# Squares queued in the first quad, weights a block ahead and a feature-major second down projection in a two-layer decoder

## The chip, the cores and the metric

The kernel runs on one core of a Trainium2 chip. The metric is device time in microseconds (us) of one execution. The engines are named as in the profile: PE is TensorE's matmuls, PEld its weight loads, DVE is VectorE, ACT is ScalarE, POOL is GpSimd, SP is SyncE, which issues most DMAs. Every engine works through its own queue in the order that was fixed when the program was built.

## The reference

A decoder trunk of two layers over 512 positions of 1024 features, in float32. Each layer adds a mixer's output and then a gated feed-forward to the residual stream x:

```
x = x + mix @ w_out[layer]
x = x + swiglu(rmsnorm(x, ffn_norm_g[layer]), w_gate_up[layer], w_down[layer])

def swiglu(h, w_gate_up, w_down):
    g, u = jnp.split(h @ w_gate_up, 2, axis=-1)
    return (jax.nn.silu(g) * u) @ w_down
...
return rmsnorm(x, final_norm_g)
```

The hidden width of the feed-forward is 2816. Layer 0 mixes with forgetting attention, layer 1 with differential attention; both add cross-attention into 256 memory tokens. The change touches neither attention.

## The kernel before

Float32 products are made of three products: an operand is split into a high part (a cast on ScalarE, `split` at L228) and the rest (a subtraction on VectorE, L229), and hi x hi, lo x hi and hi x lo are summed in PSUM. Activations lie feature-major (128 features on partitions, 512 positions along the row), in eight blocks kb; `xh`, `xl` hold the split parts of the stream.

After the mixer of a layer, `output_and_ffn` runs two parts.

`out_proj` (L588) makes the output projection in four blocks o of two feature blocks each. `project` (L187) loads the weights of a block in four chunks, splits each (`chunk`, L173; for chunks 0 and 4 the low part is added up by a DMA from POOL's queue) and issues 48 products of 512 columns. Behind them comes the block's epilogue: two adds of the residual on VectorE (L603, L604), a scaled copy on ScalarE (L608), and `Quarters.make` (L560), which forms sums and differences of quarters (s2, s3, s4) and splits all of them for the products of the feed-forward. In layer 0 the squares of the new stream are added up there as well (`squares`, L231). In layer 1 each feature block is turned to position-major rows instead, by four transposes on TensorE and a copy on ScalarE (`turn_rows`, L616), because layer 1's last norm and output are by position. `ahead`, called ahead of block 3, loads and splits the first three weight tiles of the feed-forward (`FirstThree`, L819).

`ffn` (L828) makes gate and up products in 11 groups of 256 hidden features ("quads"), each by a seven-product scheme over quarters instead of eight (`product`, L832: 24 products of 256 columns each). `first_quad` (L852) starts with the three products whose operands need no weight sums. The norm of the stream comes late, as a factor r1 that `activate` (L898) multiplies in before and after Silu. In layer 0 r1 is made by `finish_norm` (L262) from one total over partitions, issued behind the first three products; in layer 1 by `row_squares` (L622) and `norm_of_rows` (L627), issued behind the a22 product. `gate` (L904) multiplies, splits and stores the gated block `ah`, `al`.

The down projection of earlier quads fills the later ones: `down_blocks` (L961) makes eight pieces for each group of quads, `quad` (L910) places four of them between its products (`fill`). In layer 0 a piece is 12 products of 512 columns with the weights standing in the array, feature-major (L986 to L988), added to the residual by L990. In layer 1 a piece is 24 products of 256 columns with the activations standing, position-major (L977 to L979), added to the rows by L982. The last group of layer 1 is `final` (L1019): products, residual, final norm and output for four tiles of 128 positions.

The order of instructions on each engine is fixed by a list scheduler: among the instructions that are ready by its own model of time, the one written first in the program goes first. Instructions written inside `with behind(engine)` (L104) cannot stand ahead of the engine's last instruction written so far.

Of the kernel before, what the change touches and what calls it, by code (L numbers as in the profile page):

```python
# [34 lines left out]
def tile_yoco(  # L35
# [151 lines left out]
    def project(segs, gain, ah, al, outs, nkb, n=S, order=None, by_dma=()):  # L187

        starts = order or list(range(0, nkb, CK))
        for kb0 in starts:  # L190
            nk = min(CK, nkb - kb0)
            hi, lo = chunk(segs, kb0, nk, gain, kb0 in by_dma)
# [345 lines left out]
    class Quarters:  # L538


        def __init__(self, pl):
            self.sh = pl.tile([P, NP, 3 * H], F32R, tag="sh", name=nm("sh"))
            self.sl = pl.tile([P, NP, 3 * H], F32R, tag="sl", name=nm("sl"))
            self.x = pl.tile([P, 4 * D], F32, tag="res", name=nm("res"))
# [4 lines left out]
        def rows(self):  # L549
            return self.x.rearrange("p (t d) -> p t d", t=NT)  # L550
# [21 lines left out]
    class Scratch:  # L572


        def __init__(self, pl):
            self.pl, self.n = pl, 0
# [7 lines left out]
        def next_half(self):  # L584
            self.n += 1
            return self.half(("p1", "u2", "u3")[self.n % 3])

    def out_proj(l, yh, yl, order, qs, sc, ahead):  # L588

        acc = tmp("xacc")  # L590
        late, xg = [], None
        for o in range(4):
            bs = two_banks(("acc", "sc", "y", "tr")[o])
            if o == 3:
                ahead()
            project([(w_out[l], o * 256, 256)], None, yh, yl, bs, NKB, order=order, by_dma=(0, 4))
            for f in late:
                f()
# [15 lines left out]
        return acc, late  # L614

    def turn_rows(kb, xn, rows):  # L616
        b = bank("tr")
        for t in range(NT):
            pe.transpose(b[:, t * P : (t + 1) * P], xn[:, t * P : (t + 1) * P], ident)
        act.copy(rows[:, :, kb * P : (kb + 1) * P], b.rearrange("p (t c) -> p t c", c=P))  # L620

    def row_squares(rows, ss, half):  # L622
        for t in range(NT):
            q = work()
# [651 lines left out]
```

## Time and profile before

| | |
|---|---|
| median of 3 runs | 1194.24 us (1193.36 to 1194.33) |
| the profiled execution | 1194.78 us |
| its span, first to last instruction | 1193.0 us |
| granted TensorE clock, mean over the span | 0.994 |
| busy: PE, PEld, DVE, ACT, POOL | 1164.1, 1062.2, 993.7, 662.6, 158.9 us |

Busy time is the union of an engine's instructions. The profiled execution has 1.78 us around its span. A matmul's row shows its start and its modelled duration; matmuls overlap, so the time that one costs is read from its start to the start of the next.

### The profile page before, as it was taken

Reading aid. Unit: us, or ns where it says so; the run is one execution under the profiler, and the core shown is the slowest. Engines: PE = TensorE matmul, PEld = TensorE weight load, DVE = VectorE, ACT = ScalarE, POOL = GpSimd, SP = SyncE. Lnnn points to the kernel's source line nnn. Section 1 sums busy time; section 2 is a strip of 40 time slices with the busy share of each in tenths; the row PEclk is TensorE's granted clock in tenths of the full one; section 3 lists DMA queues with packets and bytes.
Section 4 is the critical chain, followed back from the end, with each engine's and each line's share of the span. In section 5 each row is a group of like instructions: output and inputs, shape, how many; then the busy total and the mean of one; then the engine's idle time right before and its main releaser. Section 6 shows DMA issues by size and latency. Waiting matters only on the chain.

```text
span 1193.0 us, 21037 instructions
## 1 busy us (share of the span) xinstructions
PE 1164.1 (98%) x7866; PEld 1062.2 (89%) x7866; DVE 993.7 (83%) x1705; ACT 662.6 (56%) x1206; POOL 158.9 (13%) x154
## 2 busy tenths in 40 slices
PE   8999999999999999999999999998999999999997
PEld 7888888789999999999987878876999999999996
DVE  5879987799987787888779999979798887877776
ACT  7658776775444333344466878887554343333334
POOL 0002001113121111110001020111221111111000
PEclk8999999999999999999999999999999999999999
DMA  7533334458777666664233335346778666665512
GB/s 239 140 88 83 78 76 103 130 128 190 187 182 167 152 156 155 155 145 120 72 109 99 86 86 148 105 111 150 159 174 199 164 151 145 158 150 146 148 54 89
DMA packets 163065, 160.46 MB, mean 134 GB/s; under 512 B 12993, under 2 KB 152698, under 8 KB 162962
## 3 DMA queue, kind: packets, MB, share of 16 engines
q1 hardware_dynamic: 136146, 130.79, 37.0%
q0 software_dynamic: 26240, 27.27, 15.8%
q8 instruction: 62, 1.02, 0.4%
q10 hardware_dynamic: 576, 1.05, 0.2%
q14 instruction: 41, 0.34, 0.1%
HBM read 142.23 MB, written 2.10 MB: 121 GB/s over the span
## 4 chain that ended last, share of the span: by engine, by line
PE 75%; DVE 13%; ACT 5%; DMA 3%; issue 2%; SPq 1%; DVEq 0%; ACTq 0%; POOL 0%; POOLq 0%
PE acc L842 4%; PE acc L841 4%; PE y L842 4%; PE y L841 4%; PE y L840 4%; PE acc L840 4%; PE tr L986 3%; PE tr L987 3%; PE tr L988 3%; PE sc L842 3%; PE sc L841 3%; PE sc L840 3%; PE tr L979 3%; PE tr L977 3%; PE tr L978 3%; PE acc L201 3%
## 5 line engine op out<-in xcount | busy, mean ns | idle before, releaser
L228 ACT CAST fhi<-raw 128x1024 fp32r<-128x1024 f32 (+1 forms) x202 | 208.2, 1034 | 277.1 <-PE sc L842 107.6
L229 DVE TENSOR_TENSOR flo<-raw,fhi 128x1024 fp32r<-128x1024 f32 (+1 forms) x202 | 241.1, 1198 | 32.7 <-ACT fhi L228 32.7
L799 POOL DMA_DIRECT2D raw<-in_w_gate_up_dram x88 | 106.3, 1420 | 467.1 <-DMA raw<-in_w_gate_up_dram 256.8
L170 ACT ACTIVATE whi<-raw,gains 128x256 fp32r<-128x256 f32 (+1 forms) x192 | 86.7, 503 | 37.3 <-PE acc L201 20.2
L171 DVE SCALAR_TENSOR_TENSOR wlo<-raw,gains,whi 128x256 fp32r<-128x256 f32 (+1 forms) x192 | 87.4, 495 | 16.5 <-ACT whi L170 14.9
L842 PE MATMUL acc<-xl,fhi 128*128 128x256 f32 x352 | 99.2, 282 | 0.0
L840 PE MATMUL acc<-xh,fhi 128*128 128x256 f32 x352 | 99.0, 281 | 0.0
L841 PE MATMUL acc<-xh,flo 128*128 128x256 f32 x352 | 98.6, 280 | 0.1
L979 PE MATMUL tr<-flo,ah 128*128 128x256 f32 x288 | 81.3, 282 | 0.0
L977 PE MATMUL tr<-fhi,ah 128*128 128x256 f32 x288 | 81.3, 282 | 0.0
L978 PE MATMUL tr<-fhi,al 128*128 128x256 f32 x288 | 81.0, 282 | 0.0
L841 PE MATMUL y<-sh,flo 128*128 128x256 f32 x256 | 72.3, 283 | 3.4 <-DVE flo L229 3.4
L842 PE MATMUL y<-sl,fhi 128*128 128x256 f32 x256 | 72.7, 284 | 0.3 <-DVE sl L229 0.2
L840 PE MATMUL y<-sh,fhi 128*128 128x256 f32 x256 | 72.2, 282 | 0.0
L986 PE MATMUL tr<-ah,fhi 128*128 128x512 f32 x176 | 69.3, 394 | 0.7 <-ACT ah L228 0.7
L987 PE MATMUL tr<-ah,flo 128*128 128x512 f32 x176 | 69.1, 393 | 0.0
L988 PE MATMUL tr<-al,fhi 128*128 128x512 f32 x176 | 68.8, 392 | 0.0
L841 PEld LDWEIGHTS acc<-xh,flo 128*128 128x128 f32 x352 | 66.5, 189 | 0.8 <-DVE flo L229 0.3
L840 PEld LDWEIGHTS acc<-xh,fhi 128*128 128x128 f32 x352 | 66.5, 189 | 0.6
L842 PEld LDWEIGHTS acc<-xl,fhi 128*128 128x128 f32 x352 | 66.4, 189 | 0.5 <-DVE xl L229 0.4
L199 PE MATMUL acc<-xh,whi 128*128 128x512 f32 x168 | 66.6, 397 | 0.2 <-DVE qk L732 0.2
L200 PE MATMUL acc<-xh,wlo 128*128 128x512 f32 x168 | 66.3, 395 | 0.0
(494 smaller groups left out, 3788.8 us busy)
## 6 DMA issues: line engine op xcount, KB each, us to landing
raw<-in_w_gate_up_dram SPq DMA_DIRECT2D x220, 256.0 KB, 3.4
raw<-in_w_gate_up_dram POOLq DMA_DIRECT2D x88, 256.0 KB, 5.8
raw<-in_w_down_dram SPq DMA_DIRECT2D x80, 256.0 KB, 3.5
raw<-in_w_out_dram SPq DMA_DIRECT2D x32, 256.0 KB, 2.7
raw<-in_a_w_in_dram SPq DMA_DIRECT2D x48, 128.0 KB, 2.4
raw<-in_w_kv_shared_dram SPq DMA_DIRECT2D x24, 256.0 KB, 3.3
raw<-in_w_mem_kv_dram SPq DMA_DIRECT2D x16, 256.0 KB, 3.3
raw<-in_a_w_in_dram SPq DMA_DIRECT2D x16, 256.0 KB, 4.0
```

Of the source, the lines that this page charges most:

```text
L228: act.copy(h, src)
L229: dve.tensor_sub(l, src, f32(h))
L799: pool.dma_start(t[:, k : k + 2], plus[:, k : k + 2], accum_op=ALU.add)
L840: pe.matmul(o, hi[:, e, uc], ah, start=u == 0 and e == 0, stop=False)
L841: pe.matmul(o, lo[:, e, uc], ah, start=False, stop=False)
L842: pe.matmul(o, hi[:, e, uc], al, start=False, stop=u == 1 and e == NP - 1)
L977: pe.matmul(o, h[:, tc_], hi[:, k], start=t % 2 == 0 and k == 0, stop=False)
L978: pe.matmul(o, l_[:, tc_], hi[:, k], start=False, stop=False)
L979: pe.matmul(o, h[:, tc_], lo[:, k], start=False, stop=t % 2 == 1 and k == nk - 1)
L986: pe.matmul(b, hi[:, k, oc], h, start=k == 0, stop=False)
L987: pe.matmul(b, lo[:, k, oc], h, start=False, stop=False)
L988: pe.matmul(b, hi[:, k, oc], l_, start=False, stop=k == nk - 1)
```

## The change

- `out_proj`: the weights of block o + 1 are loaded and split behind block o's products and ahead of its epilogue; `ahead` is called behind the weights of block 3, ahead of block 2's epilogue. Both layers keep the stream feature-major in `qs.block(kb)`; the transposes and the row squares are gone from here, and so are the squares of layer 0.
- `first_quad`: the first three products are queued behind all of TensorE's earlier instructions. The eight squares of the stream (ScalarE) are queued behind the copy of v1, with their adds on VectorE; `finish_norm` is queued behind the a22 products, in both layers.
- `down_blocks`: layer 1 takes layer 0's form, 12 products of 512 columns in a piece.
- The end of layer 1: the eight feature blocks are turned to rows there, four transposes and four copies of 128x128 each, into two tiles that take the places of `sh` and `sl`.

```
-    def project(segs, gain, ah, al, outs, nkb, n=S, order=None, by_dma=()):
+    def project(segs, gain, ah, al, outs, nkb, n=S, order=None, made=None):
...
-            hi, lo = chunk(segs, kb0, nk, gain, kb0 in by_dma)
+            hi, lo = made[kb0] if made else chunk(segs, kb0, nk, gain)
...
-        def rows(self):
-            return self.x.rearrange("p (t d) -> p t d", t=NT)
+        def make_rows(self):
+
+            return [self.pl.tile([P, 2, D], F32, tag=t, name=nm("row")) for t in ("sh", "sl")]
...
-        acc = tmp("xacc")
-        late, xg = [], None
+
+        def weights(o):
+            return {kb: chunk([(w_out[l], o * 256, 256)], kb, CK, None, kb in (0, 4)) for kb in order}
+
+        made = weights(0)
         for o in range(4):
             bs = two_banks(("acc", "sc", "y", "tr")[o])
-            if o == 3:
+            project(None, None, yh, yl, bs, NKB, order=order, made=made)
+            if o < 3:
+                made = weights(o + 1)
+            if o == 2:
                 ahead()
-            project([(w_out[l], o * 256, 256)], None, yh, yl, bs, NKB, order=order, by_dma=(0, 4))
-            for f in late:
-                f()
-            late = []
+            xg = sc.full("g")
             for j in range(2):
                 kb = 2 * o + j
-                xn = qs.block(kb) if l == 0 else sc.next_half()
-                dve.tensor_add(xn, bs[j], f32(xh[:, kb]))
-                dve.tensor_add(xn, xn, f32(xl[:, kb]))
-                if j == 0:
-                    xg = sc.full("g")
+                dve.tensor_add(qs.block(kb), bs[j], f32(xh[:, kb]))
+                dve.tensor_add(qs.block(kb), qs.block(kb), f32(xl[:, kb]))
                 g = gains[:, G_FFN[l] + kb : G_FFN[l] + kb + 1]
-                act.activation(xg[:, j], xn, AF.Copy, scale=g)
-                if l == 0:
-                    squares(xn, acc, kb == 0)
-                else:
-                    late.append(lambda kb=kb, xn=xn: turn_rows(kb, xn, qs.rows()))
+                act.activation(xg[:, j], qs.block(kb), AF.Copy, scale=g)
...
+        def turn_rows(i, rows):
+            b = bank("sc")
+            for t in range(NT):
+                pe.transpose(b[:, t * P : (t + 1) * P], qs.block(i)[:, t * P : (t + 1) * P], ident)
+            for t in range(NT):
+                act.copy(rows[t // 2][:, t % 2, i * P : (i + 1) * P], b[:, t * P : (t + 1) * P])
...
             bp1, bp2, bp3 = bank("acc"), bank("sc"), bank("y")
-            for es in (range(NP - 1), range(NP - 1, NP)):
-                product(bp1, "a11", w.w11, es)
-                product(bp2, "a12", w.w21, es)
-                product(bp3, "s4", w.w22, es)
+            with behind(pe):
+                for es in (range(NP - 1), range(NP - 1, NP)):
+                    product(bp1, "a11", w.w11, es)
+                    product(bp2, "a12", w.w21, es)
+                    product(bp3, "s4", w.w22, es)
             t1 = raw(w.b12, w.b11)
             wt3 = parts(w.t3)
-            with behind(pe):
-                if last:
-                    for f in late:
-                        f()
-                    row_squares(qs.rows(), ss, 1)
-                else:
-                    finish_norm(acc, False, bank("tr"))
...
             act.copy(v1, halves(bp3))
+            acc = tmp("xacc")
+            with behind(act):
+                for i in range(NKB):
+                    squares(qs.block(i), acc, i == 0)
...
             product(bp4, "a22", wt4)
-            if last:
-                with behind(pe):
-                    norm_of_rows(ss)
+            with behind(pe):
+                finish_norm(acc, False, bank("tr"))
...
-                if last:
-                    for t in (2 * (i % 2), 2 * (i % 2) + 1):
-                        tc_, o = slice(t * P, (t + 1) * P), b[:, (t % 2) * H : (t % 2) * H + H]
-                        for k, (h, l_) in enumerate(a):
-                            pe.matmul(o, h[:, tc_], hi[:, k], start=t % 2 == 0 and k == 0, stop=False)
-                            pe.matmul(o, l_[:, tc_], hi[:, k], start=False, stop=False)
-                            pe.matmul(o, h[:, tc_], lo[:, k], start=False, stop=t % 2 == 1 and k == nk - 1)
-                    t0 = 2 * (i % 2)
-                    dst = qs.rows()[:, t0 : t0 + 2, c * 256 : c * 256 + 256]
-                    dve.tensor_add(dst, halves(b), dst)
-                    return
...
-        final(w, blocks_of(GROUPS[-1]), qs.rows(), ring, sc)
-
-    def final(w, a, xtok, ring, sc):
+        rows = qs.make_rows()
+        for i in range(NKB):
+            turn_rows(i, rows)
+        final(w, blocks_of(GROUPS[-1]), rows, ring, sc)
+
+    def final(w, a, rows, ring, sc):
...
-                dve.tensor_add(xo[:, c], o, xtok[:, t, c])
+                dve.tensor_add(xo[:, c], o, rows[t // 2][:, t % 2, c])
```

## Rows read from the trace of the kernel before

**Rows 1.** The page, first part: busy us, share of the span, instructions.

```profile
PE 1164.1 (98%) x7866; PEld 1062.2 (89%) x7866; DVE 993.7 (83%) x1705; ACT 662.6 (56%) x1206; POOL 158.9 (13%) x154
```

**Rows 2.** Windows by stage: length, busy us of each engine (instructions), granted clock, DMA share, GB/s.

```profile
257.27:268.42 11.15, 11.15 (x49) 9.02 (x48) 10.50 (x17) 5.41 (x8) 0.86 (x1) 1.00 0.27 49
268.42:289.53 21.11, 20.96 (x172) 20.27 (x171) 19.11 (x29) 12.52 (x17) 7.24 (x6) 1.00 0.95 218
289.53:588.67 299.14, 298.46 (x2114) 279.88 (x2113) 248.98 (x265) 120.38 (x123) 44.08 (x40) 1.00 0.62 152
...
819.53:840.44 20.91, 16.88 (x76) 13.36 (x75) 14.88 (x25) 11.97 (x24) 1.74 (x2) 0.92 0.34 73
840.44:860.34 19.90, 19.86 (x167) 19.55 (x166) 15.82 (x26) 14.11 (x26) 7.24 (x6) 1.00 0.98 226
860.34:1163.96 303.62, 303.55 (x2554) 303.34 (x2553) 250.41 (x271) 122.15 (x125) 43.47 (x36) 1.00 0.60 147
1163.96:1193.00 29.04, 22.56 (x110) 18.42 (x108) 18.34 (x46) 13.53 (x33) 0.00 (x0) 0.93 0.25 91
```

**Rows 3.** Windows around TensorE's longest stop in layer 1, and one of the start.

```profile
10.00:20.00 10.00, 8.04 (x51) 7.36 (x50) 6.47 (x21) 9.88 (x26) 1.28 (x5) 0.77 0.82 281
...
822.40:826.10 3.70, 0.28 (x2) 0.07 (x1) 3.70 (x8) 3.70 (x10) 0.00 (x0) 1.00 0.00 0
826.10:828.00 1.90, 1.73 (x6) 1.24 (x7) 1.90 (x4) 1.90 (x5) 0.00 (x0) 0.72 0.35 97
828.00:830.00 2.00, 2.00 (x6) 1.52 (x6) 2.00 (x4) 1.32 (x4) 0.88 (x1) 0.50 0.51 170
830.00:832.00 2.00, 2.00 (x9) 1.37 (x7) 2.00 (x4) 0.60 (x1) 0.86 (x1) 0.91 0.76 131
```

**Rows 4.** Timeline of PE: a whole down piece and the product behind it, both layers.

```profile
580.23 0.40 PE L986 MATMUL tr<-ah,fhi 128*128 128x512 f32 x1
...
583.03 0.27 PE L840 MATMUL acc<-sh,fhi 128*128 128x256 f32 x1
...
1138.41 0.28 PE L977 MATMUL tr<-fhi,ah 128*128 128x256 f32 x1
...
1141.24 0.28 PE L840 MATMUL sc<-sh,fhi 128*128 128x256 f32 x1
```

**Rows 5.** Waits of PE, 811.5 to 875: us in total, times, longest.

```profile
PE y L841 <- DVE flo L229: 3.4, 1, 3.4
...
PE tr L200 <- DMA wlo<-raw: 0.4, 1, 0.4
```

**Rows 6.** Timeline of PE: the total, transposes, and the small norm products.

```profile
277.55 1.02 PE L253 MATMUL tr<-xacc,ones 128*128 128x512 f32 x2
...
278.53 0.28 PE L840 MATMUL acc<-sh,fhi 128*128 128x256 f32 x1
...
819.53 0.60 PE L619 MATMUL tr<-ident,p 128*128 128x128 f32 x4
...
820.32 0.37 PE L840 MATMUL acc<-xh,fhi 128*128 128x256 f32 x1
...
861.78 1.05 PE L637 MATMUL tr<-work,ones 128*128 128x128 f32 x8
862.59 0.36 PE L840 MATMUL acc<-xh,fhi 128*128 128x256 f32 x1
```

**Rows 7.** The line that adds squares up: duration ns min/median/max, first and last start.

```profile
L238 DVE TENSOR_TENSOR xacc<-xacc,work x14: 683/686/692, 243.0 to 613.5; 128x512 f32<-128x512 f32 x14
```

**Rows 8.** Timeline of DVE and PE, layer 0: r1, its first use, first down product.

```profile
287.23 0.41 DVE L265 TENSOR_SCALAR r<-work 128x512 f32<-128x512 f32 x1
...
290.49 1.22 DVE L900 TENSOR_TENSOR g<-g,r 128x1024 f32<-128x1024 f32 x1
...
299.18 0.50 PE L986 MATMUL tr<-ah,fhi 128*128 128x512 f32 x1 [0.68 <-ACT ah L228]
```

**Rows 9.** Groups by line and form, ACT: busy us, mean ns; idle before.

```profile
L467 ACT CAST vp<-vmem 128x128 fp32r<-128x128 f32 x8 | 1.9, 294 | 0.1
```

More of the change, by code (lines that the diff above doesn't have):

```diff
@@ L541, in __init__ @@
         def __init__(self, pl):
+            self.pl = pl
             self.sh = pl.tile([P, NP, 3 * H], F32R, tag="sh", name=nm("sh"))
@@ L575, in __init__ @@
         def __init__(self, pl):
-            self.pl, self.n = pl, 0
+            self.pl = pl
         def half(self, tag):
@@ L613, in out_proj @@
-            qs.make(o, xg, sc.full("u").rearrange("p a c -> p (a c)")[:, : 3 * H])
[L614 to L624, printed above, removed]
-            act.activation(q, rows[:, t, half * S : half * S + S], AF.Square, accum_out=ss[:, half, t : t + 1])
@@ L627, in norm_of_rows @@
-    def norm_of_rows(ss):
-        r = tmp("nrm", (P, NT))
-        dve.tensor_add(ss[:, 0], ss[:, 0], ss[:, 1])
-        rstd(ss[:, 0], NT, D, r)
-        dve.tensor_scalar_mul(r, r, undo_k(D))
-        d = work().rearrange("p (t c) -> p t c", c=P)
-        b = bank("tr")
-        for t in range(NT):
-            dve.tensor_scalar_mul(d[:, t], ident, r[:, t : t + 1])
-            pe.matmul(b[:, t * P : (t + 1) * P], ones, d[:, t], start=True, stop=True)
-        act.copy(r1, b)
+                dve.tensor_add(qs.block(kb), bs[j], f32(xh[:, kb]))
@@ L826, in __init__, with ffn @@
             self.w11, self.w21, self.w22 = (ring.parts(t) for t in (self.raw11, self.raw21, self.raw22))
-    def ffn(l, acc, last, qs, late, ring, sc, pl, ahead):
+    def ffn(l, last, qs, ring, sc, pl, ahead):
         raw, parts = ring.load, ring.parts
@@ L847, in ffn @@
         gated = {}
-        if last:
-            ss = tmp("ss", (P, 2, NT))
-            row_squares(qs.rows(), ss, 0)
+        def turn_rows(i, rows):
[4 more added lines that the diff above has]
+                act.copy(rows[t // 2][:, t % 2, i * P : (i + 1) * P], b[:, t * P : (t + 1) * P])
         def first_quad(w):
             bp1, bp2, bp3 = bank("acc"), bank("sc"), bank("y")
-            for es in (range(NP - 1), range(NP - 1, NP)):
-                product(bp1, "a11", w.w11, es)
-                product(bp2, "a12", w.w21, es)
-                product(bp3, "s4", w.w22, es)
+            with behind(pe):
[3 more added lines that the diff above has]
+                    product(bp3, "s4", w.w22, es)
             t1 = raw(w.b12, w.b11)
             wt3 = parts(w.t3)
-            with behind(pe):
-                if last:
-                    for f in late:
-                        f()
-                    row_squares(qs.rows(), ss, 1)
-                else:
-                    finish_norm(acc, False, bank("tr"))
             p1, u2, u3 = sc.half("p1"), sc.half("u2"), sc.half("u3")
@@ L972, in piece @@
                 b = bank("tr")
-                if last:
-                    for t in (2 * (i % 2), 2 * (i % 2) + 1):
-                        tc_, o = slice(t * P, (t + 1) * P), b[:, (t % 2) * H : (t % 2) * H + H]
-                        for k, (h, l_) in enumerate(a):
-                            pe.matmul(o, h[:, tc_], hi[:, k], start=t % 2 == 0 and k == 0, stop=False)
-                            pe.matmul(o, l_[:, tc_], hi[:, k], start=False, stop=False)
-                            pe.matmul(o, h[:, tc_], lo[:, k], start=False, stop=t % 2 == 1 and k == nk - 1)
-                    t0 = 2 * (i % 2)
-                    dst = qs.rows()[:, t0 : t0 + 2, c * 256 : c * 256 + 256]
-                    dve.tensor_add(dst, halves(b), dst)
-                    return
                 oc = slice((i % 2) * P, (i % 2) * P + P)
@@ L1062, in output_and_ffn @@
             ahead = []
-            acc, late = out_proj(
+            out_proj(
                 l, yh, yl, [6, 0, 2, 4], qs, sc, lambda: ahead.append(FirstThree(l, ring))
@@ L1068, in output_and_ffn @@
             ring.far = open_pool(fs, f"f{l}", "right")
-            acc = ffn(l, acc, last, qs, late, ring, sc, open_pool(fs, f"a{l}"), ahead)
+            acc = ffn(l, last, qs, ring, sc, open_pool(fs, f"a{l}"), ahead)
         if not last:
```

3 lines of the change are left out of this document (removed).

## The prediction

> **What bounds the kernel now.** I read the page's first part, then the windows by stage, then the timeline inside the stages where TensorE stops. TensorE is busy nearly all of the span [rows 1], so a change pays only by fewer or faster products, or by removing a stop of TensorE. The windows show where stops are [rows 2]. The reader is to see two pairs. Quads 1 to 10 of layer 0 (289.53 to 588.67) and of layer 1 (860.34 to 1163.96) make the same gate and up products and the same down sum; only the form of the down products differs, and the second stretch is longer. The last block of the output projection in layer 0 (257.27 to 268.42) is filled without a gap; in layer 1 the corresponding stretch (819.53 to 840.44) has TensorE idle for 4.03 us and a granted clock of 0.92. VectorE is idle there too, for 6.03 us, so it is not simply too slow: its work comes in the wrong order. The waits name it: the product of the first quad waits 3.4 us for the fhi/flo split of its weights [rows 5], at the head of TensorE's queue, and the products of block 3 stand behind it. [...]
>
> **The change, part by part.** Sums are made against the profiled execution, 1194.78 us (span 1193.0 and 1.78 around it); the median of the runs is 0.54 lower.
>
> **Down products of layer 1.** 864 products of 256 columns become 432 of 512. Busy time of TensorE in the ten quads is 303.55 us in layer 1 and 298.46 in layer 0 [rows 2]; 0.81 of the first is the eight small norm products (861.78 to 862.59) [rows 6]. 303.55 - 0.81 - 298.46 = 4.3 us. A single whole piece says less: 24 narrow products take 1138.41 to 1141.24, 2.83 us, 12 wide ones 580.23 to 583.03, 2.80 us [rows 4]; over 36 whole pieces (32 and eight half ones) that is 1.1 us. I take 4.3, since it is the same stage end to end, and keep 1.1 as the bound. The adds after them stay 40, of the same number of elements, and w_down's loads stay as they are: nothing, hidden under TensorE.
>
> The rows show 118 ns from one narrow product to the next and 233 ns for a wide one [rows 4]. [...]
>
> **The transition in layer 1.** Three edits meet here: weights of the next block are made before the block's own epilogue; the first quad's products are queued behind all of the projection, so that none can stand before block 3; and the 32 transposes, their copies and the row squares leave this stretch. TensorE's account of the gain: 4.03 us idle, 0.08 of 20.91 us for the clock, 1.7 us [rows 2, 3], and the transposes: eight of them take 819.53 to 820.32, 0.79 us, so 32 take 3.2, with their switches 3.3 us [rows 6]. Together 9.0 us. VectorE's account: it is idle 6.03 us in 819.53 to 840.44 and 4.08 in 840.44 to 860.34 [rows 2], 10.1 together; the change adds seven adds of squares of 0.69 us [rows 7], 4.8, and a norm over 512 columns, three operations of that shape and one of 0.41, 2.5 us. If the removed narrow ones count for nothing, 10.1 - 7.3 = 2.8 us are left. Those are the bounds, 2.8 and 9.0. I take 6.0, between them: VectorE's surplus can flow into the quads, where it idles 53 of 303.62 us, but the epilogue of block 3 can only start when block 3 is done, and the last block of first products waits for it. What is late next is therefore the split of block 3's operands (sl), ahead of the s4 products.
>
> **The norm product.** One total over 512 columns (277.55 to 278.53, 0.98 us) stands in place of the eight small ones, 0.81 us [rows 6]: +0.2.
>
> **Layer 0.** The squares move from the epilogue onto ScalarE's queue behind the copy of v1, and the total moves behind the a22 products, from 277.55 to about 286.7 (2.83 us of s1 products ahead of 289.53). On ScalarE the splits of wt4, t1 and quad 1's weights stand behind eight squares; on VectorE their adds. The norm r1 is done at 287.6 now and its first use starts at 290.49, so 2.9 us of cover exist; TensorE waits 0.68 us already where the first down piece needs the gated block [rows 8]. From total to r1 the operations alone need about 5 us, so r1 comes at about 291.7, 1.2 us after the present first use. Bounds: 0, where other products of quad 1 are put ahead of the down piece, and 6.3, the present 10.1 us from total to r1 begun at 286.7. I take 0.5, near the first, since layer 1 already runs with its norm that late [rows 6] and its stage is filled [rows 2]. The weights made ahead give nothing in layer 0: its blocks run without idle, hidden by the projection's own products. On SP's and POOL's queues the loads of block 3 of w_out and the two lo parts added by DMA move ahead of those of FirstThree; their 0.4 us wait [rows 5] is in the idle time above.
>
> **The end.** The transposes now stand between the last adds of the down sum and the final products, on the path: +3.3 us. Their 32 copies on ScalarE can only start when the s4 products of quad 10 release sh and sl, and hold two banks. The nearest row of 128x128 is 294 ns [rows 9], so 9.4 us against 2.8 us of the last down piece and 3.3 of transposes; final products stand ready to fill the gap. Nothing more is counted, up to 3.3 us where they do not fill it.
>
> Sum: -4.3 - 6.0 + 0.2 + 0.5 + 3.3 = -6.3, so 1188.5 for the profile and about **1188.0 us** for the runs. With each gain at its better bound and layer 0 at 0 it is 1184.5.
>
> **Rivals.** A: VectorE bounds the transition (gain 2.8, not 6.0): 1191.1 us. For it: the flo split ends TensorE's long wait there; against: 10 us of VectorE idle. B: the wide products gain 1.1 only: 1191.1 us. For it the single pieces, against it the stage. C: the copies at the end hold TensorE 3.3 us: 1191.2 us. D, on the other side: r1 is late at the first down piece of quad 1 in both layers, because the squares and their adds precede the weights' splits and TensorE's order leaves the piece in its place. Place: the wait of the first down product. Price: 6.3 us each in place of my 0.5, so 1200.0; the two waits must exceed 6.8 us together to decide. For it: 0.68 us are lost there now; against: layer 1 passes the place filled. E: the clock falls in the transposes at the end. In 10 to 20 us, where transposes and waits alternate, the granted clock was 0.77 [rows 3]; a fall cost 1.7 us at 826: 1189.7. [...] F: A and B together: 1194.3, so the change does nothing.
>
> **How the numbers follow.** Forecast 0.48, A 0.16, B 0.10, C 0.07, D 0.08, E 0.07, F 0.04. A measurement here tells about 0.2% (2.4 us) from no change. Faster takes the forecast, E, and about two thirds of A, B and C, which lie 0.7 us beyond that line: 0.77. Same takes the rest of these and F: 0.15. Slower is D: 0.08. The likeliest case has its own range of 1184.5 to 1191; the whole range, 1184.0 to 1193.0, leaves out D, F and a little of the low side.
>
> **What would show it.** Right: no TensorE idle over 2 us between the projection of layer 1 and its first quad, clock 1.00 there; the ten quads of layer 1 some 4 us shorter; 32 transposes after the last down piece, with final products among them. Wrong: a wait of the first down product of quad 1 on the gated block's split of several us (D), a wait of transposes on ScalarE's copies (C), or idle before the s4 products of layer 1 on sl of more than 4 us (A).

## The result, and the profile after

The changed kernel takes **1207.35 us** (median of four runs, 1203.79 to 1208.12); the kernel before, run beside it, 1194.03 us. The ratio is 1.0099, 95% interval 1.0085 to 1.0112: about 12 us slower by the ratio (13.3 us between these two medians), where 6 us faster were forecast. The profiled execution took 1208.12 us, with a span of 1206.0.

The first part of the page after, beside [rows 1]. TensorE has 438 instructions fewer and is nevertheless 6.4 us longer busy:

```profile
PE 1170.5 (97%) x7428; PEld 1047.9 (87%) x7428; DVE 999.4 (83%) x1707; ACT 664.8 (55%) x1221; POOL 158.3 (13%) x154
```

The windows by stage after, in the order of [rows 2] and with its columns: block 3 of the projection and first quad of layer 0; then, behind the rows left out, block 3 and first quad of layer 1; its ten quads; the end.

```profile
257.10:268.17 11.07, 11.07 (x49) 8.93 (x48) 7.39 (x13) 5.54 (x8) 0.86 (x1) 1.00 0.22 53
268.17:294.13 25.96, 24.69 (x199) 23.80 (x198) 24.16 (x36) 15.47 (x24) 7.27 (x6) 1.00 0.81 182
...
823.87:843.42 19.55, 14.19 (x51) 11.02 (x50) 13.18 (x22) 10.91 (x16) 2.93 (x3) 0.83 0.43 89
843.42:870.65 27.23, 24.33 (x173) 22.02 (x172) 24.85 (x37) 15.64 (x23) 7.24 (x6) 0.94 0.77 175
870.65:1173.04 302.39, 300.88 (x2112) 282.00 (x2112) 249.22 (x267) 121.21 (x124) 43.44 (x36) 1.00 0.59 147
1173.04:1206.00 32.96, 26.41 (x141) 21.74 (x139) 18.57 (x46) 19.19 (x65) 0.00 (x0) 0.96 0.22 80
```

The first quad of layer 1 was filled before (19.86 of 19.90 us); now it stands 2.9 us still and has a clock of 0.94. Block 3 ahead of it stands 5.4 us still, at 0.83. The end has grown by 3.9 us. The waits of TensorE from 811.5 to 890 us name the places, as [rows 5] did before:

```profile
PE tr L200 <- DMA wlo<-raw: 5.4, 1, 5.4
PE y L809 <- ACT fhi L228: 2.1, 3, 0.9
PE tr L253 <- DVE xacc L238: 0.8, 1, 0.8
PE tr L946 <- ACT ah L228: 0.6, 1, 0.6
PE acc L809 <- ACT fhi L228: 0.6, 1, 0.6
PE sc L809 <- ACT fhi L228: 0.4, 1, 0.4
```

The stop of the kernel before was a split of VectorE. In its place there is a longer one, on a low part that DMA adds up (`wlo<-raw`). Everything below it is new: the first quad waits for splits of its weights, for the sum of squares and for the gated block. The timeline of ScalarE in the first quad of layer 1 shows why:

```profile
856.60 0.59 ACT L843 COPY u<-y 128x512 f32<-128x512 f32 x1 [2.14 <-PE y L811]
857.09 0.64 ACT L234 ACTIVATE xacc<-res 128x512 f32<-128x512 f32 x1
857.62 3.75 ACT L237 ACTIVATE work<-res 128x512 f32<-128x512 f32 x7
861.27 2.92 ACT L228 CAST fhi<-raw 128x1024 fp32r<-128x1024 f32 x3
```

Eight squares stand for 4.2 us ahead of three casts of weights. TensorE's timeline there (in brackets the idle time before and what ended it) has two stops for those casts and one for the sum; the rows between are left out:

```profile
863.30 0.38 PE L809 MATMUL acc<-xh,fhi 128*128 128x256 f32 x1 [0.56 <-ACT fhi L228]
...
864.24 0.39 PE L809 MATMUL y<-sh,fhi 128*128 128x256 f32 x1 [0.56 <-ACT fhi L228]
...
865.41 1.82 PE L253 MATMUL tr<-xacc,ones 128*128 128x512 f32 x2 [0.79 <-DVE xacc L238]
```

ScalarE's queue is worked off in order here: the first cast begins at 861.27, as the last square ends (857.62 + 3.75 = 861.37).

To see where the 13 us between the two profiled spans (1206.0 and 1193.0) lie I set marks on TensorE that both kernels have, and take the time between them from the two traces:

| From the mark before to | before, us | after, us | difference |
|---|---|---|---|
| first gate/up product of layer 0 | 268.42 | 268.17 | -0.25 |
| norm's total in layer 1's attention (all of layer 0's feed-forward lies here) | 353.81 | 358.27 | +4.5 |
| first product of layer 1's output projection | 151.41 | 152.79 | +1.4 |
| last product of that projection | 66.57 | 63.81 | -2.8 |
| 168th gate/up product, as many as a quad has | 20.01 | 27.31 | +7.3 |
| last gate/up product | 300.79 | 299.78 | -1.0 |
| last product of the down pieces | 2.83 | 2.69 | -0.1 |
| last instruction of TensorE | 22.40 | 26.36 | +4.0 |

Projection and first quad of layer 1 together have become 4.5 us longer, not 6 shorter. And layer 0's 4.5 us are not all stops: it has 1848 gate and up products, the same before and after, but from the start of one to the start of the next they take 118.2 ns before and 119.6 ns after (means of all under 160 ns), 2.5 us of the 4.5. No instruction of these products was changed.

### The profile page after: what moved, and what is told of

Same layout as the page of the kernel before. It is cut to its first block, busy times and chain, and to the rows that moved or that the text cites. A ratio compares the mean times of both kernels' runs of the same rounds, so it can differ in the third digit from the quotient of the medians.

```text
span 1206.0 us, 20191 instructions
## 1 busy us (share of the span) xinstructions
PE 1170.5 (97%) x7428; PEld 1047.9 (87%) x7428; DVE 999.4 (83%) x1707; ACT 664.8 (55%) x1221; POOL 158.3 (13%) x154
## 4 chain that ended last, share of the span: by engine, by line
PE 80%; DVE 10%; ACT 4%; DMA 3%; issue 2%; SPq 0%; POOL 0%; DVEq 0%; ACTq 0%; POOLq 0%
PE tr L946 6%; PE tr L947 6%; PE tr L948 6%; PE acc L810 4%; PE acc L811 4%; PE acc L809 4%; PE y L809 4%; PE y L811 4%; PE y L810 4%; PE sc L810 3%; PE sc L811 3%; PE sc L809 3%; PE acc L201 3%; PE acc L200 3%; PE acc L199 3%
## 5 line engine op out<-in xcount | busy, mean ns | idle before, releaser
L946 PE MATMUL tr<-ah,fhi 128*128 128x512 f32 x320 | 125.6, 392 | 0.6 <-ACT ah L228 0.6
L947 PE MATMUL tr<-ah,flo 128*128 128x512 f32 x320 | 125.9, 393 | 0.0
L948 PE MATMUL tr<-al,fhi 128*128 128x512 f32 x320 | 125.1, 392 | 0.0
L170 ACT ACTIVATE whi<-raw,gains 128x256 fp32r<-128x256 f32 (+1 forms) x192 | 86.6, 503 | 39.2 <-PE acc L201 22.1
L811 PE MATMUL acc<-xl,fhi 128*128 128x256 f32 x352 | 99.6, 283 | 0.0
L948 PEld LDWEIGHTS tr<-al,fhi 128*128 128x128 f32 x320 | 60.1, 188 | 13.2
L946 PEld LDWEIGHTS tr<-ah,fhi 128*128 128x128 f32 x320 | 60.3, 188 | 11.6 <-ACT ah L228 1.0
L947 PEld LDWEIGHTS tr<-ah,flo 128*128 128x128 f32 x320 | 60.2, 188 | 10.5
```

What stands on the lines that cost most here:

```text
L170: act.activation(hi[:, k], v[:, k], AF.Copy, scale=g)
L811: pe.matmul(o, hi[:, e, uc], al, start=False, stop=u == 1 and e == NP - 1)
L946: pe.matmul(b, hi[:, k, oc], h, start=k == 0, stop=False)
L947: pe.matmul(b, lo[:, k, oc], h, start=False, stop=False)
L948: pe.matmul(b, hi[:, k, oc], l_, start=False, stop=k == nk - 1)
```

## The experiments

Fifteen kernels ran. Ratios are to the kernel before, run beside each; the changed kernel has 1.0099.

| | median, us | ratio, 95% interval |
|---|---|---|
| 1 changed, squares back | 1203.47 | 1.0076, 1.0059 to 1.0092 |
| 2 before + wide down form | 1204.14 | 1.0080, 1.0064 to 1.0095 |
| 3 before + weights ahead | 1195.62 | 1.0010, 0.9996 to 1.0023 |
| 4 changed, no queued products | 1206.37 | 1.0095, 1.0076 to 1.0114 |
| 5 changed + 64 bytes | 1202.37 | 1.0059, 1.0042 to 1.0076 |
| 6 before + 64 bytes | 1195.66 | 1.0010, 1.0000 to 1.0020 |
| 7 changed, splits first | 1212.97 | 1.0149, 1.0123 to 1.0174 |
| 8 changed, rows not turned | 1203.19 | 1.0068, 1.0044 to 1.0093 |
| 9 = 1 and 5 | 1197.34 | 1.0022, 1.0010 to 1.0033 |
| 10 = 9, no low part by DMA in block 3 | 1195.53 | 1.0005, 0.9990 to 1.0020 |
| 11 changed, 64 bytes ahead of the ring | 1196.61 | 1.0018, 1.0009 to 1.0028 |
| 12 before, its 64 bytes ahead of the ring | 1188.92 | 0.9966, 0.9953 to 0.9978 |
| 13 = 1, 11 and no low part by DMA in block 3 | 1190.91 | 0.9976, 0.9965 to 0.9987 |
| 14 = 12, no low part by DMA in block 3 | 1189.09 | 0.9960, 0.9948 to 0.9972 |
| 15 changed, 96 bytes ahead of the ring | 1203.68 | one run |

**Run 1: squares and total back.** In the changed kernel:

```
                 act.activation(xg[:, j], qs.block(kb), AF.Copy, scale=g)
+                squares(qs.block(kb), acc, kb == 0)
...
             wt3 = parts(w.t3)
+            with behind(pe):
+                finish_norm(acc, False, bank("tr"))
...
-            with behind(act):
-                for i in range(NKB):
-                    squares(qs.block(i), acc, i == 0)
...
-            with behind(pe):
-                finish_norm(acc, False, bank("tr"))
```

> The changed kernel with the eight squares of each layer back in the epilogues of the output projection, and the norm's total back behind the first three products of the first quad; weights one block ahead, queued products and the feature-major second down projection stay. Theory 1 (squares and their adds, queued on ScalarE and VectorE ahead of the first quad's weight splits, starve TensorE: +4.5 us by the first down product of layer 0, +8.1 us between the end of the projection and the first down product of layer 1): the two first quads lose these delays, the epilogues of layer 1 take 8 squares of about 0.65 us back on ScalarE, of which 0 to 3 us show; 1207.4 - 4.5 - 8.1 + 0 to 3 = 1195 to 1198 us. Theory 2 (the weights made a block ahead are what pushes the first quad's splits late): the first quads stay as they are, 1204 to 1209 us, the first down product of layer 1 about 12 us after that of the kernel before.

It gave 3.9 us back, not 9 to 12. Theory 2 is out (that mark of the first quad fell from 27.31 to 23.41 us), but theory 1 priced the squares at twice and more of what they cost. Part of the loss only moved: projection and first quad of layer 1 together are back at 86.7 us (86.6 in the kernel before), but the ten quads behind them grew from 299.8 to 302.8 us, and the first down product there now waits 1.7 us for the gated block.

**Run 2: the feature-major down form alone**, in the kernel before: layer 1 in the form of layer 0 (`qs.block`, squares in the epilogue, wide pieces), rows turned at the end, neither weights ahead nor queued products.

> The kernel before with the feature-major second down projection alone: layer 1's output projection and first quad as layer 0 of the kernel before has them (squares in the epilogue, total behind the first three products), the 32 transposes at the end; weights not ahead, products not queued. Theory 1: down form -3.4 us, end +3.9 us, transition without the 40 transposes and the norm of rows -3 to -6 us: 1188 to 1192 us, layer 0 unchanged to 0.5 us. Theory 2 (the down form or the end costs more than it was read as): 1194 to 1198 us. Theory 3 (the slower products, 119.6 against 118.2 ns, come with the feature-major form by the places of its tiles): layer 0's products at 119.6 ns again and +4 us over theory 1.

1204.14 us, 6 us above the highest of the three ranges. Of theory 3 the pace came true: layer 0, whose instructions are those of the kernel before, has products of 119.61 ns, 2.5 us. The end is 4.0 us longer, as in the changed kernel, and projection and first quad of layer 1 are 5.6 us longer by the marks, though the 32 transposes and the eight products of the norm of rows have left them: the squares now stand in the epilogues, between splits, and TensorE's first long stop there has grown to 5.0 us. The part meant to gain loses by itself, some 4 us of it by the pace.

**Run 3: the weights ahead alone**, in the kernel before.

```
...
+        made = weights(0)
         for o in range(4):
...
-            if o == 3:
+            project(None, None, yh, yl, bs, NKB, order=order, made=made)
+            if o < 3:
+                made = weights(o + 1)
+            if o == 2:
                 ahead()
-            project([(w_out[l], o * 256, 256)], None, yh, yl, bs, NKB, order=order, by_dma=(0, 4))
```

> The kernel before with nothing but the weights of the output projection made one block ahead and the first quad's loads put behind the next block's. Theory 1: layer 0 as before to 0.5 us, layer 1 has the new wait for the low parts that DMA adds (5.4 us in the changed kernel) in place of the 3.4 us wait there was: 1193 to 1197 us. Theory 2 (weights ahead delay the first quads): the first down product of each layer 4 to 8 us later than before, 1200 to 1207 us.

No change that can be measured, and products of 118.25 and 118.69 ns, as before. The time is theory 1's, its stop is not: TensorE waits for no low part in block 3 here; the stop of 3.4 us has given way to several, the longest 1.2 us. So weights made a block ahead do not by themselves make the low part late; the stop of over 5 us stands only where they and the feature-major form come together (0.5 us in run 2). The slow pace came neither with this part nor by chance of a run: up to here every kernel with the wide form had 119.6, every kernel without it 118.2 to 118.7.

**Run 4: no order on the first products** (`with behind(pe):` taken from around them in the changed kernel).

> The changed kernel without the order that holds the first quad's first 48 products behind the last product of the output projection. On TensorE 7 of them then come ahead of the products that wait 5.4 us for a low part in block 3. Theory 1: these 7 x 0.12 = 0.8 us fill part of that wait and the slow stretch behind it stays: 1205.5 to 1207 us. Rival (the queued products are what lets TensorE run dry and its clock fall there): the wait goes below 3 us with no halved clock behind it, 1201 to 1203.5 us.

1206.37, no difference to the changed kernel that its interval could tell. The stop fell from 5.4 to 2.6 us, a new one of 1.7 stood before it, and the granted clock over the span was 0.993, against 0.992 in the changed kernel.

What differs for these products of layer 0, when none of their instructions does, is where the tiles lie. The change drops two small tiles of the norm of rows, 64 bytes in each partition, from a pool that is laid out ahead of the feed-forward pools, so the operands, residual, scratch and gated tiles of the feed-forward layers and the ring with three of its four pairs of split weights moved down by 64 bytes. `xh` and `xl`, which lie ahead of it, stayed, and so did the fourth pair, whose pool is laid out from the other end of the partition. Runs 5 and 6 try that.

**Run 5: the bytes put back.**

```
+    pool.memset(tmp("pad", (P, 16)), 0.0)
```

> The changed kernel with one unused tile of 64 bytes a partition in the pool of small tiles, which puts the tiles of both feed-forward layers back at the addresses that they have in the kernel before (the change drops the two small tiles of the norm of rows, 64 bytes, and so moved all of them down by 64). Theory P (the products' pace, 119.6 against 118.2 ns, follows these addresses and nothing else of the change): 118.2 to 118.3 ns in layer 0 and 118.7 in layer 1, -2.5 and -1.6 us, the same stops as in the changed kernel: 1202 to 1203.5 us. Rival (the pace follows the program, its order or its length): 119.6 ns in both, 1206 to 1208 us.

118.23 ns in layer 0, 118.27 in layer 1 (0.4 better than expected), and 5.0 us: theory P.

**Run 6: the same line in the kernel before.**

> The kernel before with the same unused tile of 64 bytes, which moves its feed-forward tiles up by 64 bytes: to the same remainder by 128 as those of the changed kernel. Theory P, if the remainder by 128 decides: 119.6 ns in both layers, +2.5 and +1.6 us, 1198 to 1199.5 us with not an instruction of its work changed. Rival: 118.2 and 118.7 ns stay, 1194 to 1195 us.

Products of 118.7 ns in both layers, 1195.66 us: the remainder by 128 does not decide. The pace changes (118.23 to 118.72 in layer 0), but this is another place with another pace.

**Run 7: the weights' splits ahead of the squares**, in the changed kernel.

```
             act.copy(v1, halves(bp3))
+            bp7 = bank("acc")
+            product(bp7, "s3", wt3)
+            dve.tensor_add(w.raw21, w.raw21, w.raw11)
+            wt4 = parts(w.raw21)
+            pt1 = parts(t1)
             acc = tmp("xacc")
             with behind(act):
                 for i in range(NKB):
                     squares(qs.block(i), acc, i == 0)
...
```

> The changed kernel with the eight squares of the first quad queued behind the splits of its last two weights instead of ahead of them. Theory 1 (the squares make these splits late): the two stops of 0.8 us at 863.3 and 864.2 us go, as do the stops of 1.1 and 0.9 us at 288 and 298 us; the total comes 2 us later: 1203.5 to 1206 us. Rival (the norm is what is late: the later total gives it back at the total and at the first down products): 1207 to 1210 us.

1212.97 us: the rival, and theory 1 in its simple form is wrong. The splits' stops go (the first quad is 5.2 us shorter), but the last step of r1 begins 2 us later (874.86 against 872.89) and TensorE now stops where it is used. TensorE's waits from 811.5 to 903 us there:

```profile
PE tr L200 <- DMA wlo<-raw: 5.3, 1, 5.3
PE tr L947 <- ACT ah L228: 2.6, 1, 2.6
PE acc L810 <- DVE flo L229: 1.3, 3, 0.6
PE tr L947 <- DVE res L951: 1.2, 1, 1.2
```

The 2.6 us are the first down product waiting for the gated block. Neither place tried in the first quad is good for the squares: ahead of the splits they starve TensorE at once, behind them the norm is late.

**Run 8: rows not turned.** The 32 transposes and their copies left out of the changed kernel; the final sums read the residual as it lies.

> The changed kernel without the 32 transposes at the end and their 32 copies; the final sums read the residual as it lies, so the output is that of rows that were not turned. Theory: the whole difference of the last stretch, 26.4 against 22.4 us from the last down piece to TensorE's last product, is these transposes: -4.0 us, 1203 to 1204 us. Rival (the transposes run beside waits for the final weights): the last stretch keeps at least 1.5 of the 4 us, above 1204.9 us.

1203.19 us; the last stretch, from the last down piece to TensorE's last instruction, is 22.40 us again. Its window from the last down piece to the end, to be laid beside the last row of the windows after:

```profile
1170.98:1200.00 29.02, 22.52 (x110) 18.56 (x108) 18.27 (x46) 13.63 (x33) 0.00 (x0) 0.97 0.24 91
```

26.41 against 22.52 us busy: the transposes are work of TensorE, not waiting. In the changed kernel TensorE is busy in all of the 26.4 us from the last down piece to its last instruction.

**Run 9: runs 1 and 5 together.**

> The changed kernel with both earlier edits: the squares and the total as layer 0 of the kernel before has them, and the 64 unused bytes that put the feed-forward tiles back at their addresses. If the two terms are independent they add: 1207.4 - 3.9 (squares) - 5.0 (addresses) = 1198.5 us (1197.5 to 1199.5), products at 118.2 to 118.3 ns, and what is left over the kernel before is the 4.0 us of the transposes at the end. If the squares' gain only came from the addresses' change of the stalls, 1200 to 1203 us.

1197.34: they add, a little better than expected (the squares are worth 5.0 us at these places).

**Run 10: and no low part by DMA in block 3.**

```
-            return {kb: chunk(..., kb in (0, 4)) for kb in order}
+            return {kb: chunk(..., o < 3 and kb in (0, 4)) for kb in order}
```

> As the kernel with both edits (squares in the epilogues, 64 bytes), and the weights of the last block of each output projection are split on ScalarE and VectorE alone, with no low part added by DMA. Theory W (the 5.4 us stop of TensorE in the last block of layer 1 is the low part's long way: a late load, ScalarE's negative copy, the add by DMA): the stop goes below 2.5 us and the halved clock behind it with it, -3 to -5 us, 1193.5 to 1196 us. Rival V (VectorE is what bounds the transition, and two more subtractions of 128x512 push the splits of the first three weights): the stop moves into the first quad, -1 to +2 us, 1197 to 1201 us.

The long stop is gone. TensorE's account from the projection's start to its last product, run 9 and then run 10:

```profile
774.00:838.13 64.13, 58.59 (x257) 45.54 (x256) 50.93 (x107) 46.15 (x92) 8.46 (x9) 0.95 0.52 124
```

```profile
772.00:828.52 56.52, 56.43 (x262) 44.12 (x261) 46.94 (x101) 42.63 (x85) 6.66 (x7) 1.00 0.51 125
```

64.1 us become 56.5, filled, at a granted clock of 1.00 in place of 0.95. But 3.0 of the 7.6 to 8.3 us come back in the first quad (24.84 to 27.85 us by the marks), and the runs, which spread from 1191.97 to 1199.94, give 1.8 us at the median; the intervals of runs 9 and 10 overlap. Theory W for the stop, and half of rival V for what follows.

**Run 11: only the ring of weights moved** (and the gated tiles that lie behind it). In the changed kernel, ahead of the ring's tiles, and with no instruction added:

```
             self.near, self.far, self.n, self.m = near, None, 0, 0
+            near.tile([P, 16], F32, tag="pad", name=nm("pad"))
```

> The changed kernel with 64 unused bytes ahead of the ring of the split weights alone: the weights, the gated values and nothing else are at the addresses of the kernel before; the operands that lie in the feed-forward pool (sums of quarters, residual) stay where the change put them, and no instruction is added. Theory D (the pace follows the distance of the weights from the moving operand): products that read the normalized input go back from 119.4-120.3 to 117.0-117.9 ns, those that read the sums of quarters move from 119.2 ns by as much as their distance now differs; all products 118 to 118.6 ns, 1202 to 1204 us. Rival (the address of the sums and the residual decides): products of the normalized input stay at 119.4 to 120.3 ns, 1206 to 1208 us.

1196.61 us, 10.7 us below the changed kernel, and well below what theory D expected. Products of `xh` and `xl` went to 117.2 to 117.5 ns, those of the sums of quarters, which had 118.9 to 119.4 in every kernel so far, to 116.3. One quad's products can be followed in TensorE's timeline (the first and the third row of each view start 24 products, and the row behind ends them). Before, after, and this run:

```profile
330.04 0.28 PE L840 MATMUL y<-xh,fhi 128*128 128x256 f32 x1
...
332.84 0.28 PE L840 MATMUL sc<-xh,fhi 128*128 128x256 f32 x1
...
337.04 0.27 PE L840 MATMUL acc<-sh,fhi 128*128 128x256 f32 x1
...
339.90 0.40 PE L986 MATMUL tr<-ah,fhi 128*128 128x512 f32 x1
```

```profile
332.21 0.28 PE L809 MATMUL y<-xh,fhi 128*128 128x256 f32 x1
...
335.08 0.29 PE L809 MATMUL sc<-xh,fhi 128*128 128x256 f32 x1
...
339.35 0.28 PE L809 MATMUL acc<-sh,fhi 128*128 128x256 f32 x1
...
342.23 0.39 PE L946 MATMUL tr<-ah,fhi 128*128 128x512 f32 x1
```

```profile
331.29 0.28 PE L810 MATMUL y<-xh,fhi 128*128 128x256 f32 x1
...
334.09 0.28 PE L810 MATMUL sc<-xh,fhi 128*128 128x256 f32 x1
...
338.29 0.28 PE L810 MATMUL acc<-sh,fhi 128*128 128x256 f32 x1
...
341.04 0.39 PE L947 MATMUL tr<-ah,fhi 128*128 128x512 f32 x1
```

24 products of `xh`: 2.80, 2.87, 2.80 us. 24 of `sh`: 2.86, 2.88, 2.75 us. The duration printed for one product, 0.28 us, does not show it; only the distance of the starts does.

The fourth pair of weights is a control inside each trace. Taken apart by the addresses in the built programs, products of `xh` and `xl` with the three pairs that moved took 119.9 ns in the changed kernel, 117.0 in run 5 and 116.8 in run 11; with the fourth pair, which did not move, 119.7, 119.4 and 119.4 ns. So it is mainly the place of a product's own weights that counts, and not something that slows the whole stage.

**Run 12: the kernel before at those places**: its two small tiles are taken from the head of the ring's pool; nothing else differs.

```
+            self.ss = near.tile([P, 2, NT], F32, tag="ss", name=nm("ss"))
+            self.nrm = near.tile([P, NT], F32, tag="nrm", name=nm("nrm"))
...
-            ss = tmp("ss", (P, 2, NT))
+            ss = ring.ss
```

> The kernel before with its two small tiles of the norm of rows (64 bytes) taken from the head of the ring's pool instead of the pool of small tiles, so that every feed-forward tile lies where the changed kernel with the 64 bytes ahead of the ring has it; not an instruction of its work differs. Theory D (the distance from weights to moving operand sets the pace): 117.0 ns in both layers instead of 118.2 and 118.7, -2.3 and -3.1 us: 1188.5 to 1190 us, so that the change of work itself costs 7 us (1196.6 against 1189.5). Rival (the 117.0 ns came with something else of the changed kernel): 1193 to 1196 us, and the change of work costs 1 to 2 us.

1188.92 us, 116.9 and 116.8 ns: theory D's number, and the fastest median of all. The kernel before was not at its best place either.

**Run 13: the changed kernel with all three repairs.**

> The changed kernel with squares and total back in the epilogues and behind the first products, no low part of the last block added by DMA, and the 64 bytes ahead of the ring alone. From the kernel with the same two edits and the earlier places (1195.5 us, 118.25 ns) only the pace should move, to 117.0 ns: -4.6 us: 1190 to 1192 us, faster than the kernel before as it was, and no faster than the kernel before at these places if theory D holds.

1190.91 us, faster than the kernel before as it was and not faster than run 12, both as expected.

**Run 14: run 12 with block 3's weights split on ScalarE and VectorE.**

> The kernel before at the ring's places of the run beside it, with the last block's weights split on ScalarE and VectorE alone. Theory W (the DMA-added low part is what the last block waits for): 2 to 5 us below that run, 1184 to 1188 us. Rival V (here TensorE's long stop, 3.4 us at 826, waits for VectorE's split of a first-quad weight, and two more subtractions make it longer): 0 to 3 us above that run.

1189.09, no difference to run 12 that can be measured, which is the near edge of rival V. In the kernel before the long stop is VectorE's (3.4 us at 824.3 here too), so taking the DMA away helps only where the stop is the DMA's.

**Run 15: 96 bytes ahead of the ring.**

> The changed kernel with 96 instead of 64 unused bytes ahead of the ring; one look. The products of the normalized input then have weights and operand a multiple of 1024 bytes apart, as those of the sums of quarters have it in the kernels before and after (119.2 ns there). Theory D with that distance taken modulo 1024: products of the normalized input at 119.0 to 119.5 ns. Rival (another address rule): anything else, as 116 to 118 or over 120 ns. No forecast for the products of the sums, whose distance (96) no run has shown.

Products of `xh` and `xl` at 119.4 to 119.9 ns, by a little outside the band that theory D named, and of the sums at 118.2. So the rule "distance modulo 1024" is not shown (over the three moved pairs alone these products took 119.8 ns, the sums at the same remainder in the changed kernel 119.6, so it is not refuted either); that the pace changes with where weights and moving operand lie to each other is (117.2 to 117.5 ns with the weights moved by 64 bytes against `xh` and `xl` in run 11, 119.4 to 119.9 by 96).

## Why the prediction was wrong

With the tiles at the same places, but for the scratch tiles of layer 1, the change of work costs 1.0018 / 0.9966 = 1.0052 (run 11 by run 12), 6 us; at the changed kernel's own places 12 us. The traces of runs 12 and 11 give the account at equal places, with the same marks as above: layer 0 +2.1, attention +0.55, projection of layer 1 -3.9, first quad +5.9, ten quads -1.6, end +3.9, and +0.8 ahead of layer 0's feed-forward, 7.8 us between these two executions. Of the signs named for a right forecast only the last was seen: transposes behind the last down piece, with final products among them.

**Down form, -4.3.** Right in sign, a little large. Before, 864 narrow products at 119.2 ns make 103.0 us; after, 432 wide ones at 230.6 ns make 99.6: -3.4 us. The 4.3 was the difference of two stages, and 0.8 of it was not form: 1680 gate and up products were 0.47 ns slower in layer 1 (118.70 against 118.23), which I read as an effect of the down products. The narrow form alone does not make it: in runs 6 and 12 layer 1 has that form too and was no slower than layer 0 (118.7 in both, and 116.8 against 116.9). An effect of places is likely, since the scratch tiles of layer 1 lie elsewhere than those of layer 0, but no run shows it.

**Transition of layer 1, -6.0 of a range of 2.8 to 9.0.** This step failed, sign included: +2.0 at equal places, +4.5 as measured. I took the idle time of TensorE there as something that goes away once the order is changed, and VectorE's 6.03 us of idle time as room for it. [rows 3] already spoke against that: VectorE and ScalarE were busy in all of the 3.70 us of the stop. VectorE's idle time lay behind it, 6.03 us of 8.44:

```profile
832.00:840.44 8.44, 8.00 (x34) 6.50 (x35) 2.41 (x5) 1.88 (x2) 0.00 (x0) 1.00 0.18 33
```

Two things replaced the stop. First, the raw weights of block 3 came late, so ScalarE stood idle 2.98 us and then made the negative copies behind two scaled copies; the adds by DMA followed at 828.50 and 829.90 and TensorE waited until 832.64. In POOL's queue I had placed these adds in "the idle time above" at 0.4 us; they became the longest stop (rows from the timelines of ScalarE, POOL and TensorE):

```profile
824.14 0.62 ACT L181 CAST whi<-raw 128x512 fp32r<-128x512 f32 x1 [2.98 <-DMA raw<-in_w_out_dram]
...
826.34 1.33 ACT L606 ACTIVATE g<-res,gains 128x512 f32<-128x512 f32 x2
827.58 0.62 ACT L180 ACTIVATE wlo<-raw 128x512 fp32r<-128x512 f32 x1
...
828.50 0.88 POOL L182 DMA_DIRECT2D wlo<-raw  x1 [0.59 <-DVE u L567]
829.90 0.86 POOL L182 DMA_DIRECT2D wlo<-raw  x1 [0.52 <-issue]
...
832.64 0.79 PE L200 MATMUL tr<-yh_b,wlo 128*128 128x512 f32 x1 [5.36 <-DMA wlo<-raw]
```

Run 10 shows it: without them the projection is filled. Why they come this late only with weights ahead and the feature-major form together (runs 2 and 3) stays open. Second, VectorE's and ScalarE's surplus could not "flow into the quads": the squares and the splits that feed TensorE share two queues worked off in order (the cast at 861.27 began as the last of the squares ended). Runs 1 and 9 price it at 4 to 5 us for both layers, run 7 shows that the other order is worse. The clock's 1.7 us in the sum are what [rows 3] give too: 1.90 us at 0.72, 2.00 at 0.50 and 2.00 at 0.91 are as much as about 3.4 us at a granted clock of 0.50.

**The norm product, +0.2.** No experiment isolates it. The two products of the total stand 1.1 us in layer 0 at a granted clock of 1.00 and, behind the stops of 864, 1.8 us in layer 1 at one of 0.58.

**Layer 0, +0.5 of 0 to 6.3.** Too near the low bound: pace aside, the stage grew by 1.9 us, most of it stops (TensorE's idle time in it rose from 0.8 to 2.1 us, the longest 0.97 us at 288.27, for VectorE's split of a weight), and the last step of r1 began at 293.40 in place of the 291.7 worked out, because VectorE puts splits of 1.22 us between the operations of the norm. The other 2.5 us are places. That the norm is "that late" in layer 1 before spoke for nothing: there four of the eight squares were done by 827.7 us and four by 853.6, on ScalarE, and the same instructions took the sums, with no adds on VectorE.

**End, +3.3.** Mis-sized: 4.0 us, by run 8. Eight transposes took 0.79 us at 1173.04; those that come later in fours take 0.36 to 0.41 us, and the final product behind them needs 0.31 us and more instead of 0.23 to the next.

**Weights ahead, nothing in layer 0, part of the 6.0 in layer 1.** Nothing in either: run 3.

**The queued products** cost and give nothing measurable (run 4).

**Rival D** had the right sign and the right matter, a norm that comes late since the squares stand ahead of the splits. It named the wrong place and price: the first down product waits 0.6 us in layer 1 and not at all in layer 0, not 6.3; most is lost at the splits and at the sum. A's sign, TensorE waiting on `sl`, is not among the waits above. B, and with it F, had the down form at 1.1 us; it gained 3.4. C and E did not come: through the transposes, 1173.04 to 1181.60, TensorE was busy all the time at a granted clock of 1.00. The 0.77 that E read in 10 to 20 us stood over 48 products, with transposes at its start alone.

```profile
1173.04:1181.60 8.56, 8.56 (x53) 6.83 (x52) 4.83 (x6) 8.30 (x33) 0.00 (x0) 1.00 0.19 63
```

**What no step had**: that removing two tiles of together 64 bytes moves the tiles of the feed-forward layers, and that this costs 5 us, as much as any term of the sum.

In ratios the whole difference of 0.99% divides into places 0.40 (run 5), squares and total 0.37 (run 9 against 5), turning the rows 0.31 (run 8), the late low parts 0.17 (run 10 against 9), and the down form's gain of 3.4 us, -0.28: 0.97. Each term is uncertain by about 0.2, and the account is not closed: it gives no credit for the 3.4 us stop and the 3.3 us of transposes that left the transition, so the waits that took their place must have cost about as much beyond the 0.17. Those not named one by one stay open.

## What to carry to other kernels

Work taken from a stage in which TensorE waited was no gain here, since the queues that it was moved into had no room at that moment (the first quad of layer 1 grew from 19.90 to 27.23 us): read which engine feeds TensorE in the new place, and what stands behind the moved work there. When instructions that were not touched change their pace, compare the addresses of their tiles before looking for a cause in the schedule; a tile added or dropped ahead of a pool shifts everything behind it (64 bytes here, and 119.6 ns in place of 118.2 in layer 0). Before crediting a change, run both kernels at the same places: here that halved the loss (12 us, 6 at equal places), and re-placing the old kernel alone gained more than any edit of its work (ratio 0.9966, run 12).

## What the runs showed of the hardware

The distance of the starts of products of 256 columns, each with weights of its own, ran from 115.1 to 120.3 ns over these kernels (means by operands), at a granted clock of 1.00 in the quads. With nothing changed but the places of tiles in the partition, the mean of all went from 119.6 to 117.0 ns (changed kernel and run 11) and from 118.5 to 116.8 (kernel before and run 12). Moved by 0, 64 and 96 bytes against `xh`, the weights gave 119.4 to 120.3, 117.2 to 117.5 and 119.4 to 119.9 ns; against the sums of quarters 119.2, 116.3 and 118.2. The two operands are not all of it: in run 12, where weights and sums lie as in run 11, the sums took 116.3 in layer 0 but 115.3 in layer 1, which has other scratch places and narrow down products between; and the products of the sums with the fourth pair of weights, of which neither moved between the changed kernel and run 11, went from 117.8 to 118.7. Which rule of addresses stands behind it is open. The 3696 products of a run times 2.6 ns are 9.6 us, most of the 10.7 us between the changed kernel and run 11.

A stop of TensorE of 5.4 us was followed by 5.8 us at a granted clock of 0.50, in the windows of that stop, of what follows, and of the rest of the block (columns as in [rows 2]). The length of the stop does not fix that: the stop of 3.7 us before had gone with about as much as 3.4 us at 0.50 [rows 3], and so did a stop of 5.46 us in run 11 (a granted clock of 0.93 over the 25.00 us from 815).

```profile
826.93:832.64 5.71, 0.35 (x2) 0.00 (x0) 5.34 (x10) 4.20 (x8) 2.72 (x3) 0.91 0.73 118
832.64:838.40 5.76, 5.76 (x14) 4.50 (x15) 5.72 (x9) 2.35 (x4) 0.00 (x0) 0.50 0.41 111
838.40:843.42 5.02, 5.02 (x24) 4.08 (x23) 1.36 (x4) 1.57 (x2) 0.00 (x0) 1.00 0.00 0
```
